# One-hots of four tokens in two VectorE operations, 64 expert tiles projected in the routing stage

## The chip, the core and the metric

The kernel runs on one core of one Trainium2 chip. A core has five engines with a queue each, and each works through its queue in order: TensorE (PE, with its weight loads shown apart as PEld), VectorE (DVE), ScalarE (ACT), GpSimd (POOL) and SyncE (SP), which here only issues transfers. The metric is the device time of one execution in microseconds.

## The reference

The program is two transformer blocks on 512 tokens of 1024 values. Only the last part of the second block, `peer`, is touched: each token picks, in each of 8 heads, 16 of 16384 experts by two lists of 128 sub-keys, and adds up what these experts give.

```
q = (xb @ w_query).reshape(TOKEN_BLOCK, P_HEADS, 2, P_HALF)
s = jnp.einsum('thpk,hpnk->thpn', q, sub_keys)
sv, si = lax.top_k(s, P_TOPK)
cand = sv[:, :, 0, :, None] + sv[:, :, 1, None, :]
cidx = si[:, :, 0, :, None] * N_KEYS + si[:, :, 1, None, :]
fv, fpos = lax.top_k(cand.reshape(...), P_TOPK)
eidx = jnp.take_along_axis(cidx.reshape(...), fpos, axis=-1)
g = jax.nn.softmax(fv, axis=-1)
act = jax.nn.gelu(jnp.einsum('td,thkd->thk', xb, u_tab[eidx]))
return jnp.einsum('thk,thkd->td', g * act, v_tab[eidx])
```

## The kernel before

Tokens stand in 4 tiles of 128. Tile 0 (NG = 1) is "gathered": for each of its 128 choices the rows of the tables `peer_u` and `peer_v` are fetched by an indirect DMA and used on VectorE (256 steps, `g_load` and `g_use`, lines 1607 to 1621). The other 3 tiles (ND = 3) are computed dense: for each of 128 tiles of 128 experts, all 384 tokens are projected (24 matmuls of 384 columns in three-term split precision, `mm3`, lines 196 to 198), put through gelu, weighted by a dense matrix of routing weights, and multiplied with the `peer_v` tile into PSUM (`acc`).

Three stages follow one another.

The **top-16 stage** ends with VectorE picking the 16 best sub-keys (lines 1536 to 1540).

The **routing stage** makes the weights, and beside it TensorE already projects NPRE of the 128 expert tiles. Its parts:
- `fill(n)` projects one expert tile ahead ("fill tile"): a load of `ur`, two casts `uh` on ScalarE (line 1720), two differences `ul` on GpSimd (line 1723), 24 matmuls, a gelu, and a write of the result `ga` to DRAM (`gad`, line 1745).
- `route(T)` finds the final 16 of each head for token tile T: a chain of about 80 VectorE instructions, with one exponential on ScalarE.
- `scatter(T)`, for the 3 dense tiles, turns the choices (row i, column j and weight of each) into dense weights. For each group of 4 tokens (32 groups a tile, 96 in all) it builds one-hot rows of i and j (`hots`, line 1898, two VectorE instructions), multiplies one of them with the weight in three bf16 parts (`part`, line 1904, on VectorE and GpSimd; `weigh`, line 1909, on ScalarE), forms the outer products (`outer`, line 1917, 12 matmuls of 128 x 128) and copies them to `stg` (`keep`, line 1924). After 16 groups `stg` is written to the DRAM tensor `gd_p` in four transfers (line 1944).

The **late stage** loops over the 128 expert tiles: it loads `vr` and the weights `gt` (line 1641, from `gd_p`), projects the tiles that are not done yet (`uh`, `ul` by lines 186 and 192), multiplies with `vr`, and spreads the 256 gather steps over the loop; a tile that is done ahead carries only GPRE = 0.36 of another's share of them.

The order in the routing stage is set by a planner, `Agenda`. Each piece of work is given an engine, a cost in us, the pieces that it needs and an aim (the time at which it should run). The planner plays this through and emits on each engine, whenever it is free, the ready piece with the earliest aim; buffers (`bufs`: two pairs `uh`/`ul`, three `ur`, OHB = 3 sets of one-hots, two `sc` banks) hold a piece back until an older user is through. What it emits is the order of each queue; on the chip the queues wait for one another by semaphores.

Of the kernel before, what the change touches and what calls it, by code (L numbers as in the profile page):

```python
# [1477 lines left out]
NPRE = 52  # L1478
LEAD, EACH, TOTAL = 36.0, 70.0, 275.0
# [11 lines left out]
def peer(kk, out):  # L1491
# [206 lines left out]
    quad = stp.tile([128, 128, 4], BF, name="quad")  # L1698
    nc.gpsimd.tensor_copy(quad, iota[:, :, None].to_broadcast([128, 128, 4]))
    ag = Agenda()  # L1700
    bufs = {"ur": 3, "u": 2, "mm": 3, "ga": 4, "sc": 2, "oh": OHB, "stg": 2}
    def fill(n):
        e, aim = pre[n], n * TOTAL / NPRE
        st = {}

        def load():
            st["raw"] = u_load(e)

        if n < len(early):
            st["raw"], ld = early[n], None  # L1710
        else:
            ld = ag.add("SP", 0, load, aim=aim - 12, nbytes=128 * D * 4, ring=[("ur", n)])
        los = []
        for q in range(2):
            sl = slice(q * 4, q * 4 + 4)

            def hi(sl=sl, q=q):
# [8 lines left out]
            t = ag.add("ACT", 0.52, hi, [ld], aim, ring=ring)
            if n % LOPOOL:
                los.append(ag.add("DVE", 0.62, lambda f=lo: f(nc.vector), [t], aim, ring=ring))
            else:
                los.append(ag.add("POOL", 1.25, lambda f=lo: f(nc.gpsimd), [t], aim, ring=ring))  # L1730
        for s_ in range(4):
            def mms(s_=s_):
                if s_ == 0:
# [5 lines left out]
            t = ag.add("PE", 0.96, mms, [los[s_ // 2]], aim + 3 + s_, ring=[("u", n), ("mm", n)])  # L1739
# [4 lines left out]
        t = ag.add("ACT", 0.38, act, [t], aim + 6, ring=[("mm", n), ("ga", n)])
        ag.add("SP", 0, lambda: nc.sync.dma_start(gad[:, e, :], st["ga"]), [t], aim + 6,
               nbytes=128 * ND * 128 * 4, ring=[("ga", n)])

    def route(T, aim, span, start):
# [26 lines left out]
        step("DVE", 1.2, begin)  # L1775
# [16 lines left out]
        for i in range(0, 8, 2):  # L1792
            step("DVE", 1.4, lambda i=i: best(i))
# [8 lines left out]
        step("DVE", 0.35, weights)  # L1802
# [46 lines left out]
        step("DVE", 2.7, column)  # L1849
        step("DVE", 1.15, lambda: pick(st["ge"], st["ge"], st["di"]))  # L1850
        step("DVE", 1.15, lambda: pick(st["tm"], st["tm"], st["s2"]))
        step("DVE", 1.4, lambda: tree(st["res"][:, 0, :], st["ge"]))
# [10 lines left out]
    def scatter(T, done, aim, span):  # L1863
# [9 lines left out]
        def turned():  # L1873

            v = st["ps"][:, :384].rearrange("p (a n) -> p a n", a=3)
            st["ij"] = tk.tile([128, 2, 128], BF, name="ij", tag="ij", bufs=1)
# [1 line left out]
            w = [tk.tile([128, 128], BF, name=f"w{c}", tag=f"w{c}", bufs=1) for c in range(3)]
            r = [tk.tile([128, 128], FT, name=f"wr{c}", tag=f"wr{c}", bufs=1) for c in range(2)]
            st["w"] = w + r[1:]  # L1880
            nc.scalar.copy(r[0], v[:, 2, :])
# [8 lines left out]
        ready = ag.add("DVE", 0.8, lambda: None, [ready], aim)  # L1890
        evs = []
        for g in range(32):
            t0 = aim + span * g / 32
# [36 lines left out]
            t = []  # L1930
            for c, lo, hi, eng in ((1, 0, WPOOL, "POOL"), (1, WPOOL, 4, "DVE"), (0, 0, 4, "DVE"), (2, WACT, 4, "DVE")):
                if lo < hi:
                    cost = 0.05 + 0.27 * (hi - lo) if eng == "POOL" else 0.07 + 0.07 * (hi - lo)
                    t.append(ag.add(eng, cost, lambda f=part, c=c, lo=lo, hi=hi, e=eng:
                                    f(nc.gpsimd if e == "POOL" else nc.vector, c, lo, hi), [u], t0, ring=[o1]))
            if WACT:
                t.append(ag.add("ACT", 0.3 * WACT, weigh, [u], t0, ring=[o1]))
# [220 lines left out]
```

## Time and profile before

| | us |
|---|---|
| median of 3 runs | 2541.49 (2539.76 to 2541.68) |
| the profiled execution | 2541.76 |
| its span in the trace | 2540.0 |
| routing stage, first fill matmul to first `acc` matmul | 1284.7 to 1691.5 |
| late stage, to the last gather steps | 1691.5 to 2490 |
| TensorE busy in the span | 2442.7 (96%) |
| VectorE busy in the span | 1910.8 (75%) |
| GpSimd busy in the span | 679.6 (27%) |

All times of the trace count from the start of the span. A matmul's duration in the trace contains its latency; consecutive ones overlap, so what it costs TensorE is the distance from its start to the next start. "Busy" is the share of time in which at least one instruction of the engine is under way. [...]

### The profile page before, as it was taken

What the parts mean: (1) busy time and instruction counts of PE and PEld (TensorE: products, weight loads), DVE (VectorE), ACT (ScalarE), POOL (GpSimd) and SP (SyncE); (2) the same over time, 40 slices, a digit from 0 to 9 for tenths busy, and PEclk for the clock granted to TensorE, in tenths of its full rate; (3) what the DMA queues carried; (4) which work ended last, traced back from release to release, by engine and by line L of the source; (5) the groups of instructions that cost most, each with busy time, mean ns of one, the idle gap of its engine ahead of it and who ended that gap; (6) DMA issues with size and microseconds to landing.
All of it is one profiled execution on the core that took longest, in us unless ns stands there. A gap on an engine that the chain in (4) does not pass through costs nothing.

```text
span 2540.0 us, 36035 instructions
## 1 busy us (share of the span) xinstructions
PE 2442.7 (96%) x12979; PEld 2121.0 (84%) x12979; DVE 1910.8 (75%) x3886; ACT 1079.0 (42%) x1887; POOL 679.6 (27%) x599
## 2 busy tenths in 40 slices
PE   5989999999999999999989999999999999999998
PEld 4778877887888887778888888988888888888887
DVE  7655655676665565576899998849889889999987
ACT  3444544442332365565236676832332223322333
POOL 3110010120000020004335565544333333433330
PEclk9999999999999999999999999999999999999999
DMA  7533243546554222224133454499999999999992
GB/s 251 150 123 108 84 150 112 175 142 207 179 185 137 76 74 76 67 68 156 61 95 100 174 185 158 150 346 361 336 347 333 331 346 337 341 334 335 348 351 95
DMA packets 295715, 506.84 MB, mean 200 GB/s; under 512 B 20871, under 2 KB 193521, under 8 KB 292209
## 3 DMA queue, kind: packets, MB, share of 16 engines
q1 hardware_dynamic: 257104, 367.96, 44.1%
q0 software_dynamic: 36864, 134.23, 14.1%
q8 instruction: 102, 1.67, 0.3%
q10 hardware_dynamic: 1568, 2.35, 0.3%
q14 instruction: 77, 0.62, 0.1%
HBM read 460.70 MB, written 43.78 MB: 199 GB/s over the span
## 4 chain that ended last, share of the span: by engine, by line
PE 80%; DVE 14%; DMA 2%; issue 2%; ACT 2%; POOL 0%; DVEq 0%; ACTq 0%; SPq 0%; POOLq 0%
PE mm L197 16%; PE mm L198 16%; PE mm L196 16%; PE acc L196 7%; PE acc L198 7%; PE acc L197 7%; PE sc L1917 3%; DVE oh L1904 2%; DVE oh L1898 2%; PE av L813 1%; PE sc L926 1%; PE av L940 1%; DMA adraw<-in_w_ada 1%; PE sc L794 1%; PE sc L1549 1%
## 5 line engine op out<-in xcount | busy, mean ns | idle before, releaser
L196 PE MATMUL mm<-hh,wh 128*128 128x512 f32 (+2 forms) x976 | 373.3, 384 | 5.0 <-ACT hh L519 3.4
L197 PE MATMUL mm<-hl,wh 128*128 128x512 f32 (+2 forms) x976 | 371.6, 381 | 2.4 <-DVE hl L331 2.4
L198 PE MATMUL mm<-hh,wl 128*128 128x512 f32 (+2 forms) x976 | 370.3, 380 | 1.4 <-DVE wl L192 1.4
L196 PE MATMUL mm<-hh,uh 128*128 128x384 f32 x1024 | 353.6, 345 | 4.5 <-ACT uh L186 4.5
L198 PE MATMUL mm<-hh,ul 128*128 128x384 f32 x1024 | 347.5, 339 | 0.2
L197 PE MATMUL mm<-hl,uh 128*128 128x384 f32 x1024 | 346.8, 339 | 0.0
L186 ACT CAST wh<-wraw 128x1024 fp32r<-128x1024 f32 (+1 forms) x170 | 173.6, 1026 | 364.0 <-PE mm L197 331.8
L196 PE MATMUL acc<-vh,wgh 128*128 128x512 f32 x768 | 301.1, 392 | 0.0
L198 PE MATMUL acc<-vh,wgl 128*128 128x512 f32 x768 | 300.1, 391 | 0.0
L197 PE MATMUL acc<-vl,wgh 128*128 128x512 f32 x768 | 298.6, 389 | 0.0
L186 ACT CAST vh<-vr 128x1024 fp32r<-128x1024 f32 x128 | 135.2, 1056 | 235.6 <-PE acc L198 230.0
L192 DVE TENSOR_TENSOR wl<-wraw,wh 128x1024 fp32r<-128x1024 f32 x135 | 171.6, 1272 | 78.5 <-ACT wh L186 71.8
L1607 POOL DMA_INDIRECT gr<-in_peer_v,widx x128 | 159.0, 1242 | 252.3 <-DVE gacc L1621 214.6
L1592 ACT ACTIVATE ga<-mm 128x384 f32<-128x384 f32 x128 | 64.8, 506 | 370.4 <-PE mm L198 357.2
L1607 POOL DMA_INDIRECT gr<-in_peer_u,widx x128 | 152.1, 1188 | 242.4 <-DVE gacc L1613 221.0
L196 PEld LDWEIGHTS mm<-hh,wh 128*128 128x128 f32 (+1 forms) x976 | 183.2, 188 | 39.2 <-ACT hh L519 3.9
L197 PEld LDWEIGHTS mm<-hl,wh 128*128 128x128 f32 (+1 forms) x976 | 183.6, 188 | 36.2 <-DVE hl L331 3.4
L198 PEld LDWEIGHTS mm<-hh,wl 128*128 128x128 f32 (+1 forms) x976 | 183.7, 188 | 35.1 <-DVE wl L192 1.8
L196 PEld LDWEIGHTS mm<-hh,uh 128*128 128x128 f32 x1024 | 196.2, 192 | 8.2 <-ACT uh L186 5.2
L197 PEld LDWEIGHTS mm<-hl,uh 128*128 128x128 f32 x1024 | 195.3, 191 | 3.4
L198 PEld LDWEIGHTS mm<-hh,ul 128*128 128x128 f32 x1024 | 194.5, 190 | 0.9 <-DVE ul L192 0.9
L1723 POOL TENSOR_TENSOR ul<-ur,uh 128x512 fp32r<-128x512 f32 x104 | 146.2, 1418 | 130.5 <-ACT uh L1720 124.2
(500 smaller groups left out, 5094.8 us busy)
## 6 DMA issues: line engine op xcount, KB each, us to landing
ur<-in_peer_u_t SPq DMA_DIRECT2D x128, 512.0 KB, 6.0
vr<-in_peer_v SPq DMA_DIRECT2D x128, 512.0 KB, 5.3
wraw<-in_w_fc SPq DMA_DIRECT2D x32, 1024.0 KB, 5.6
adraw<-in_ada_w SPq DMA_DIRECT2D x96, 256.0 KB, 3.0
gd_p<-stg SPq DMA_DIRECT2D x24, 1024.0 KB, 7.0
gt<-gd_p SPq DMA_DIRECT2D x64, 384.0 KB, 7.0
wraw<-in_w_in SPq DMA_DIRECT2D x33, 512.0 KB, 3.8
adraw<-in_w_ada SPq DMA_DIRECT2D x64, 256.0 KB, 2.8
```

The source lines that it names most:

```text
L186: nc.scalar.copy(hi, view)
L192: eng.tensor_tensor(lo, view, hi, OP.subtract)
L196: nc.tensor.matmul(out, a[0], b[0], start=first, stop=False)
L197: nc.tensor.matmul(out, a[0], b[1], start=False, stop=False)
L198: nc.tensor.matmul(out, a[1], b[0], start=False, stop=last)
L794: nc.tensor.matmul(sc[:, i * n:(i + 1) * n], qp[g, hh][:, q0:q0 + 128], k_[:, :n], start=a == 0, stop=a == 1)
L1592: nc.scalar.activation(ga, ps, AF.Gelu)
L1607: nc.gpsimd.indirect_dma_start(out=r, out_offset=None, in_=A[tab], in_offset=bass.IndirectOffsetOnAxis(ap=widx[t][:, k:k + 1], axis=0))
L1723: eng.tensor_tensor(st["u"][1][:, sl, :], st["raw"][:, sl, :], st["u"][0][:, sl, :], OP.subtract)
L1898: nc.vector.tensor_tensor(o[i], quad, st["ij"][:, i, None, g * 4:g * 4 + 4].to_broadcast([128, 128, 4]), OP.is_equal)
L1904: eng.tensor_tensor(o[2 + c][:, :, lo:hi], o[0][:, :, lo:hi], w, OP.mult)
L1917: nc.tensor.matmul(ps[:, q * 128:(q + 1) * 128], o[2 + c][:, :, q], o[1][:, :, q], start=c == 0, stop=c == 2)
```

## The change

The one-hots of a group of 4 tokens are held as two pairs of tokens, with the two tokens of a pair innermost, for i and j together. One VectorE instruction of 1024 elements per partition compares them (`hots`), a second of 1536 elements multiplies all three weight parts (`parts`); `part` and `weigh`, and with them GpSimd's and ScalarE's share, are gone. In `outer` the unweighted one-hot of i is now the stationary operand and the weighted one of j streams; the step between its columns is 4 bytes where it was 8. The differences `ul` of the fill tiles move from GpSimd to VectorE. 64 tiles instead of 52 are projected in the routing stage; the first 16 have aims 4.2 us apart. Token tile 0 is routed last instead of second. Most costs that the planner is given are new numbers too.

```diff
@@
-NPRE = 52
-LEAD, EACH, TOTAL = 36.0, 70.0, 275.0
+NPRE = 64
+LEAD, EACH, TOTAL = 36.0, 100, 310
+NLEAD, PACE = 16, 4.2
...
-OHB, WACT, WPOOL = 3, 2, 2
-GPOS = 1
+OHB = 3
+GPOS = 3
...
-    quad = stp.tile([128, 128, 4], BF, name="quad")
-    nc.gpsimd.tensor_copy(quad, iota[:, :, None].to_broadcast([128, 128, 4]))
+    twice = stp.tile([128, 128, 2], BF, name="twice")
+    nc.gpsimd.tensor_copy(twice, iota[:, :, None].to_broadcast([128, 128, 2]))
...
+    def fill_aim(n):
+
+        return n * PACE if n < NLEAD else NLEAD * PACE + (n - NLEAD) * (TOTAL - NLEAD * PACE) / (NPRE - NLEAD)
+
     def fill(n):
-        e, aim = pre[n], n * TOTAL / NPRE
+        e, aim = pre[n], fill_aim(n)
...
-            t = ag.add("ACT", 0.52, hi, [ld], aim, ring=ring)
-            if n % LOPOOL:
-                los.append(ag.add("DVE", 0.62, lambda f=lo: f(nc.vector), [t], aim, ring=ring))
-            else:
-                los.append(ag.add("POOL", 1.25, lambda f=lo: f(nc.gpsimd), [t], aim, ring=ring))
+            t = ag.add("ACT", 0.62, hi, [ld], aim, ring=ring)
+            los.append(ag.add("DVE", 0.7, lo, [t], aim, ring=ring))
...
-            st["ij"] = tk.tile([128, 2, 128], BF, name="ij", tag="ij", bufs=1)
-            nc.scalar.copy(st["ij"], v[:, 0:2, :])
...
+            ij = st["ij"] = tk.tile([128, 64, 2, 2], BF, name="ij", tag="ij", bufs=1)
+            w3 = st["w3"] = tk.tile([128, 64, 3, 2], BF, name="w3", tag="w3", bufs=1)
...
+            def of(v, g):
+                return v[:, 2 * g:2 * g + 2, :, None, :].to_broadcast([128, 2, v.shape[2], 128, 2])
+
             def hots(g=g):
...
-                for i in range(2):
-                    nc.vector.tensor_tensor(o[i], quad, st["ij"][:, i, None, g * 4:g * 4 + 4].to_broadcast([128, 128, 4]),
-                                            OP.is_equal)
...
-            def part(eng, c, lo, hi, g=g):
...
-                eng.tensor_tensor(o[2 + c][:, :, lo:hi], o[0][:, :, lo:hi], w, OP.mult)
-
-            def weigh(g=g):
...
-                for q in range(WACT):
-                    nc.scalar.activation(o[4][:, :, q], o[0][:, :, q], AF.Copy,
-                                         scale=st["w"][3][:, g * 4 + q:g * 4 + q + 1])
+                o = st["oh", g] = stp.tile([128, 2, 2, 128, 2], BF, name="oh", tag="oh", bufs=OHB)
+                nc.vector.tensor_tensor(o, twice[:, None, None, :, :].to_broadcast([128, 2, 2, 128, 2]), of(st["ij"], g),
+                                        OP.is_equal)
+
+            def parts(g=g):
+                o = st["ow", g] = stp.tile([128, 2, 3, 128, 2], BF, name="ow", tag="ow", bufs=OHB)
+                nc.vector.tensor_tensor(o, st["oh", g][:, :, 1, None, :, :].to_broadcast([128, 2, 3, 128, 2]),
+                                        of(st["w3"], g), OP.mult)
...
-                        nc.tensor.matmul(ps[:, q * 128:(q + 1) * 128], o[2 + c][:, :, q], o[1][:, :, q],
+                        nc.tensor.matmul(ps[:, q * 128:(q + 1) * 128], o[:, q // 2, 0, :, q % 2], w[:, q // 2, c, :, q % 2],
                                          start=c == 0, stop=c == 2)
...
-            u = ag.add("DVE", 0.74, hots, [ready], t0, ring=[o1])
...
-            t = ag.add("PE", 0.68, outer, t, t0, ring=[o1, o2])
+            u = ag.add("DVE", 0.7, hots, [ready], t0, ring=[o1])
+            t = ag.add("DVE", 0.97, parts, [u], t0, ring=[o1])
+            t = ag.add("PE", 0.72, outer, [t], t0, ring=[o1, o2])
```

The places where the queues differ most follow, as the instructions stand on each engine.

VectorE at the start of the routing stage, before: `sv` and `si` are the top-16 work, `h2r` an unrelated sum, `cand` the first piece of `route`.

```order
L1681 TENSOR_TENSOR h2r_10156<-h2r_10156,sc 128x512
L1539 MAX sv_10173<-s_11137 128x8
L1761 CAST si_10175<-si_10175 128x256
L1540 MAX_INDEX si_10177<-sv_10173,s_11137 128x8
L1768 TENSOR_TENSOR cand<-sv_10171 128x8x16
```

The same place now:

```order
L1681 TENSOR_TENSOR h2r_10156<-h2r_10156,sc 128x512
L1539 MAX sv_10170<-s_11137 128x8
L1727 TENSOR_TENSOR ul<-ur,uh 128x512
L1540 MAX_INDEX si_10174<-sv_10170,s_11137 128x8
L1727 TENSOR_TENSOR ul<-ur,uh 128x512
L1681 TENSOR_TENSOR h2r_10156<-h2r_10156,sc 128x512
L1762 CAST si_10175<-si_10175 128x256
L1769 TENSOR_TENSOR cand<-sv_10171 128x8x16
```

The first `ul` of the first fill tile stands behind all but one of the top-16 instructions; before, it was GpSimd's, which had nothing else to do.

VectorE on one group of 4 tokens late in the stage, before: `oh_15799` and `oh_15800` are the one-hots of i and j, the next three the weighted parts.

```order
L1898 TENSOR_TENSOR oh_15799<-quad_11149,ij_14702 128x512
L1898 TENSOR_TENSOR oh_15800<-quad_11149,ij_14702 128x512
L1904 TENSOR_TENSOR oh_15802<-oh_15799,w1_14705 128x128x2
L1904 TENSOR_TENSOR oh_15801<-oh_15799,w0_14704 128x512
L1904 TENSOR_TENSOR oh_15803<-oh_15799,w2_14706 128x128x2
```

The same place now, with the two `ul` of a fill tile between the groups:

```order
L1727 TENSOR_TENSOR ul_15456<-ur_15292,uh_15455 128x512
L1906 TENSOR_TENSOR ow_15476<-oh_15465,w3_14463 128x1536
L1727 TENSOR_TENSOR ul_15456<-ur_15292,uh_15455 128x512
L1901 TENSOR_TENSOR oh_15508<-twice_11149,ij_14462 128x1024
L1906 TENSOR_TENSOR ow_15510<-oh_15508,w3_14463 128x1536
```

Five VectorE instructions a group became two larger ones, and the fill tiles' `ul` joined the queue.

SyncE at the end of the routing stage, before: `gd_p<-stg` writes the dense weights, `gt<-gd_p` is the first read of them, `gad<-ga` and `ur` belong to fill tiles.

```order
L1944 DMA gd_p<-stg 128x2048
L1745 DMA gad<-ga 128x384
L1509 DMA ur<-in_peer_u_t 128x1024
L1944 DMA gd_p<-stg 128x2048
L1745 DMA gad<-ga 128x384
L1509 DMA ur<-in_peer_u_t 128x1024
L1745 DMA gad<-ga 128x384 x3
L1509 DMA ur<-in_peer_u_t 128x1024 x2
L1638 DMA vr<-in_peer_v 128x1024
L1641 DMA gt<-gd_p 128x6x128
```

The same place now:

```order
L1934 DMA gd_p<-stg 128x2048
L1509 DMA ur<-in_peer_u_t 128x1024 x2
L1746 DMA gad<-ga 128x384
L1509 DMA ur<-in_peer_u_t 128x1024
L1746 DMA gad<-ga 128x384 x2
L1934 DMA gd_p<-stg 128x2048 x4
L1638 DMA vr<-in_peer_v 128x1024
L1641 DMA gt<-gd_p 128x6x128
```

The last four writes of the weights stood among fill tiles; now they stand together, directly ahead of the first read. TensorE's queue has the matching move: behind the last outer product stood seven whole fill tiles (168 matmuls) and the late stage's first two projections (48 matmuls); now all 64 fill tiles stand ahead of the last seven groups (84 matmuls), and only the 48 matmuls follow before the first `acc`.

## Rows read from the trace of the kernel before

**Rows 1.** Stretches: us; busy us and instructions by engine, PEclk, DMA share, GB/s

```profile
1285.00:1645.00 360.00, 334.38 (x2232) 316.95 (x2232) 335.76 (x942) 245.87 (x440) 203.54 (x187) 0.98 0.44 149
1645.00:1690.00 45.00, 40.26 (x223) 38.79 (x222) 4.28 (x6) 16.41 (x31) 21.12 (x18) 0.96 0.88 317
1690.00:2490.00 800.00, 800.00 (x3942) 711.66 (x3941) 722.14 (x1019) 242.13 (x348) 305.25 (x250) 1.00 0.97 341
```

**Rows 2.** Timeline of TensorE, fill matmuls: start us, us, engine, line, operation

```profile
1284.73 0.42 PE L196 MATMUL mm<-hh,uh 128*128 128x384 f32 x1
...
1673.68 0.34 PE L196 MATMUL mm<-hh,uh 128*128 128x384 f32 x1
...
1675.59 0.34 PE L198 MATMUL mm<-hh,ul 128*128 128x384 f32 x1
```

**Rows 3.** Timeline of TensorE: outer products with six fill matmuls between

```profile
1626.53 1.58 PE L1917 MATMUL sc<-oh 128*128 128x128 bf16 x12
...
1628.99 1.58 PE L1917 MATMUL sc<-oh 128*128 128x128 bf16 x12
```

**Rows 4.** Instructions of the tile `acc`: ns min/median/max, first to last start us

```profile
L196 PE MATMUL acc<-vh,wgh x768: 387/389/478, 1691.5 to 2530.3; 128*128 128x512 f32 x192
```

**Rows 5.** Timeline of TensorE, three pauses: [idle before, who ended it]

```profile
1319.43 0.47 PE L1871 MATMUL sc<-ident,res 128*128 128x128 f32 x1 [4.87 <-DVE res L1841]
...
1322.08 0.52 PE L197 MATMUL mm<-hl,uh 128*128 128x384 f32 x1
...
1685.27 0.44 PE L196 MATMUL mm<-hh,uh 128*128 128x384 f32 x1 [3.44 <-ACT uh L186]
```

**Rows 6.** Groups of VectorE, 1285 to 1645 us: count | busy us, mean ns

```profile
L1898 DVE TENSOR_TENSOR oh<-quad,ij 128x512 bf16<-128x512 bf16 x192 | 101.3, 576 | 8.8 <-PE sc L1917 8.1 <-POOL oh L1904 0.5
L1904 DVE TENSOR_TENSOR oh<-oh,w 128x256 bf16<-128x256 bf16 x192 | 83.1, 448 | 0.0
L1904 DVE TENSOR_TENSOR oh<-oh,w 128x512 bf16<-128x512 bf16 x96 | 55.9, 582 | 0.0
```

**Rows 7.** Timeline, VectorE alone, then beside GpSimd

```profile
1327.55 0.74 DVE L1898 TENSOR_TENSOR oh<-quad,ij 128x512 bf16<-128x512 bf16 x2
...
1397.12 2.76 POOL L1723 TENSOR_TENSOR ul<-ur,uh 128x512 fp32r<-128x512 f32 x2 [0.90 <-ACT uh L1720]
1397.23 2.93 DVE L1898 TENSOR_TENSOR oh<-quad,ij 128x512 bf16<-128x512 bf16 x2
```

**Rows 8.** Chain of waits: a 2048-element bf16 operation of VectorE: start us, us

```profile
1339.93 1.14 DVE tm L1812
```

**Rows 9.** Groups of VectorE, 1690 to 2490 us: two float32 differences

```profile
L192 DVE TENSOR_TENSOR vl<-vr,vh 128x1024 fp32r<-128x1024 f32 x122 | 148.8, 1220 | 11.7 <-ACT vh L186 11.0 <-DMA vr<-in_peer_v 0.7
L192 DVE TENSOR_TENSOR ul<-ur,uh 128x512 fp32r<-128x512 f32 x143 | 98.3, 687 | 44.1 <-ACT uh L186 43.6 <-DMA vr<-in_peer_v 0.5
```

**Rows 10.** Timeline at the stage's start: GpSimd's first `ul`, VectorE's last top-16 instruction

```profile
1284.86 2.54 POOL L1723 TENSOR_TENSOR ul<-ur,uh 128x512 fp32r<-128x512 f32 x2 [25.59 <-ACT uh L1720]
...
1293.49 0.28 DVE L1540 FIND_INDEX8 si<-sv,s 128x8 uint32<-128x128 f32 x1
```

**Rows 11.** ScalarE's copy of the outer products, 1285 to 1676 us

```profile
L1924 ACT COPY stg<-sc 128x512 f32<-128x512 f32 x96 | 106.0, 1111 | 47.8 <-PE sc L1917 47.2
```

**Rows 12.** Transfers of the tile `gd_p`, writes and reads: issue to landing, us

```profile
DMA to landing us min/median/max: 3.9/7.0/15.0
```

**Rows 13.** Timeline: the first read of `gd_p`, and VectorE's first use of it

```profile
1678.41 0.61 SPq L1641 DMA_DIRECT2D gt<-gd_p  x1
...
1690.05 0.55 DVE L1989 TENSOR_TENSOR gt<-gt,ga 128x384 f32<-128x384 f32 x1
```

**Rows 14.** Weight loads of the outer products (line 1917): ns min/median/max

```profile
L1917 PEld LDWEIGHTS <-oh x1152: 112/117/138, 1333.6 to 1646.4; 128*128 128x128 bf16 x192
```

**Rows 15.** Stretches of the late stage with the most bytes; columns as in rows 1

```profile
1690.00:1730.00 40.00, 40.00 (x207) 36.75 (x206) 39.28 (x65) 13.54 (x21) 17.53 (x14) 1.00 1.02 375
...
2410.00:2450.00 40.00, 40.00 (x202) 35.74 (x201) 37.29 (x46) 10.84 (x16) 17.58 (x14) 1.00 1.06 375
```

More of the change, by code (lines that the diff above doesn't have):

```diff
@@ L1738, in mms @@
                            k == 0, k == KD - 1)
[L1739 removed]
+            t = ag.add("PE", 1.05, mms, [los[s_ // 2]], aim + 3 + s_, ring=[("u", n), ("mm", n)])
         def act():
             st["ga"] = u_gelu(st["ps"])
[L1744 removed]
+        t = ag.add("ACT", 0.5, act, [t], aim + 6, ring=[("mm", n), ("ga", n)])
         ag.add("SP", 0, lambda: nc.sync.dma_start(gad[:, e, :], st["ga"]), [t], aim + 6,
@@ L1773, in begin @@
             st["fp"] = tk.tile([128, 8, 16], U32, name="fp", tag="fp", bufs=1)
-        step("DVE", 1.2, begin)
+        step("DVE", 1.3, begin)
         def best(i0):
@@ L1792, in route @@
         for i in range(0, 8, 2):
-            step("DVE", 1.4, lambda i=i: best(i))
+            step("DVE", 2.3, lambda i=i: best(i))
         def weights():
@@ L1800, in weights @@
             nc.vector.tensor_copy(st["pb"].rearrange("p (k h) -> p h k", h=8), st["fp"])
-        step("DVE", 0.35, weights)
+        step("DVE", 0.75, weights)
         step("ACT", 1.5, lambda: nc.scalar.activation(st["g"], st["g"], AF.Exp))
@@ L1807, in rows @@
             nc.vector.tensor_tensor(st["ge"], st["pb"][:, None, :].to_broadcast([128, 16, 128]), wide[0], OP.is_ge)
-        step("DVE", 1.15, rows)
+        step("DVE", 1.22, rows)
         def pick(out, t, v):
@@ L1817, in offset @@
             pick(st["tm"], st["ge"], dst)
-        step("DVE", 1.15, offset)
+        step("DVE", 1.22, offset)
         def norm():
@@ L1832, in norm @@
             nc.vector.tensor_copy(st["s2"], st["si2"][:, 1].rearrange("p h r -> p r h"))
-        step("DVE", 1.0, norm)
+        step("DVE", 1.7, norm)
         def tree(out, src):
@@ L1847, in column @@
             nc.vector.tensor_tensor(st["tm"], st["pb"][:, None, :].to_broadcast([128, 16, 128]), wide[1], OP.is_equal)
[L1849 to L1852, printed above, removed]
+        step("DVE", 3.1, column)
+        step("DVE", 1.22, lambda: pick(st["ge"], st["ge"], st["di"]))
+        step("DVE", 1.22, lambda: pick(st["tm"], st["tm"], st["s2"]))
+        step("DVE", 1.6, lambda: tree(st["res"][:, 0, :], st["ge"]))
         def end():
@@ L1856, in end @@
             routed[T] = st["res"]
-        step("DVE", 1.4, end)
+        step("DVE", 1.6, end)
         for i, (eng_, cost, fn) in enumerate(steps):
@@ L1875, in turned @@
             v = st["ps"][:, :384].rearrange("p (a n) -> p a n", a=3)
-            st["ij"] = tk.tile([128, 2, 128], BF, name="ij", tag="ij", bufs=1)
-            nc.scalar.copy(st["ij"], v[:, 0:2, :])
[L1878 to L1881, printed above, removed]
-            for c in range(2):
-                nc.vector.tensor_copy(w[c], r[c and 1])
-                nc.vector.tensor_tensor(r[1], r[c and 1], w[c], OP.subtract)
-            nc.vector.tensor_copy(w[2], r[1])
+            ij = st["ij"] = tk.tile([128, 64, 2, 2], BF, name="ij", tag="ij", bufs=1)
+            w3 = st["w3"] = tk.tile([128, 64, 3, 2], BF, name="w3", tag="w3", bufs=1)
+            r = [tk.tile([128, 64, 2], FT, name=f"wr{c}", tag=f"wr{c}", bufs=1) for c in range(2)]
+            for c in range(2):
+                nc.scalar.copy(ij[:, :, c, :], v[:, c, :].rearrange("p (n t) -> p n t", t=2))
+            nc.scalar.copy(r[0], v[:, 2, :].rearrange("p (n t) -> p n t", t=2))
+            for c in range(2):
+                nc.vector.tensor_copy(w3[:, :, c, :], r[c and 1])
+                nc.vector.tensor_tensor(r[1], r[c and 1], w3[:, :, c, :], OP.subtract)
+            nc.vector.tensor_copy(w3[:, :, 2, :], r[1])
         s0 = sc0 + a * 33
@@ L1889, in scatter @@
         ready = ag.add("ACT", 0.7, turned, [first], aim, ring=[("sc", s0)])
-        ready = ag.add("DVE", 0.8, lambda: None, [ready], aim)
+        ready = ag.add("DVE", 1.3, lambda: None, [ready], aim)
         evs = []
@@ L1928, in scatter @@
             o1, o2 = ("oh", n), ("sc", s0 + 1 + g)
-            u = ag.add("DVE", 0.74, hots, [ready], t0, ring=[o1])
[L1930 to L1937, printed above, removed]
-            t = ag.add("PE", 0.68, outer, t, t0, ring=[o1, o2])
+            u = ag.add("DVE", 0.7, hots, [ready], t0, ring=[o1])
+            t = ag.add("DVE", 0.97, parts, [u], t0, ring=[o1])
+            t = ag.add("PE", 0.72, outer, [t], t0, ring=[o1, o2])
             r = ("stg", 2 * a + g // 16)
-            evs.append(ag.add("ACT", 0.48, keep, [t], t0, ring=[o2, r]))
+            evs.append(ag.add("ACT", 1.1, keep, [t], t0, ring=[o2, r]))
             if g % 16 == 15:
```

11 lines of the change are left out of this document (3 added, 8 removed).

## The prediction

> **What bounds the kernel now.** I read the table of stretches first. In the late stage TensorE is busy 800 of 800 us: there only fewer matmuls help. In the routing stage TensorE has 334 of 360 us, VectorE 336 and GpSimd 204, so neither of the two main queues is full, and each waits for the other at times [rows 1]. Next come the distances on TensorE's timeline. Eleven consecutive fill matmuls start 1675.59 - 1673.68 = 1.91 us apart, 0.1736 us each [rows 2], so a fill tile of 24 costs 4.17 us. From one group's outer products to the next, with six fill matmuls between, it is 2.46 us [rows 3]; less 6 x 0.1736 that leaves 1.42 us for a group, 0.118 a matmul.
>
> The routing stage runs from the first fill matmul, 1284.73 [rows 2], to the first `acc` at 1691.5 [rows 4]: 406.8 us. TensorE's work in it is 52 x 24 + 48 = 1296 fill matmuls, 225.0 us, and 96 x 1.42 = 136.3 us of outer products: 361.3. The remaining 45.5 us are some 3 us of transposes and, for the rest, waiting: for `route`, which also leaves TensorE at half clock for a while (0.52 us a fill matmul for 0.34), for one-hots, and at the end for `uh` [rows 5].
>
> **The frame of the sum.** Twelve more tiles bring 288 x 0.1736 = 50.0 us of matmuls into the routing stage and take the same out of the late stage. On a busy TensorE that cancels. So time after = 2541.76 + (X - 45.5) + Y, with X the new remainder of the routing stage and Y new waiting of TensorE in the late stage. The profiled execution is 0.27 us above the median, and I take that off at the end.
>
> **VectorE's work.** The one-hots go: 101.3 + 83.1 + 55.9 = 240.3 us [rows 6]. Two operations of 512 took 0.74 us with GpSimd idle and 2.93 us beside GpSimd's `ul` [rows 7], so part of those 240 us was mutual hindrance, which ends, as no GpSimd tensor operation is left in the stage. For the new ones: 0.37 us per 512 elements [rows 7] and 1.14 us for 2048 bf16 elements [rows 8] give a slope of 0.26 per 512. That makes `hots` (1024) about 0.63 and `parts` (1536) 0.88: 1.51 us a group, 145 us for 96. The upper bound is float32 at about one element a cycle: 1220 ns for 1024, 687 for 512 [rows 9], so 1220 + 1753 = 2.97 us a group, 285 us. I take 1.51, since the nearest rows are bf16 with the same kind of broadcast operand. The fill tiles' `ul` cost 128 x 0.687 = 88 us more. VectorE: 336 - 240 + 145 + 88 = 329 us against 361.3 + 50.0 = 411 us of TensorE. TensorE is now the slower queue by far, so most waits for one-hots inside the stage should go. ScalarE loses `weigh` and keeps the copy of 1.11 us a group [rows 11], under the 1.42.
>
> What speaks against the price is the innermost run of two. [...]
>
> **Outer products.** Their step between columns falls from 8 to 4 bytes. The weight loads take 117 ns each [rows 14], which is the pace of 118: these seem to bound the group, not the 128 streamed columns. I keep 1.42 us. The other end is the pace of fill matmuls scaled to 128 columns, 0.1736 / 3 = 0.058: 1152 x (0.118 - 0.058) = 69 us less. Upwards I see no reason, as the load has the same 128 columns and a smaller step.
> [...]
>
> **X, term by term.**
> - Transposes: 3 us.
> - Start. GpSimd did the first `ul` at 1284.86, at once; VectorE's last top-16 instruction runs until 1293.8 [rows 10]. The first `ul` now stands behind that work, and each third matmul needs it, so TensorE stops after the first ones: about 1285.2 to 1293.2, 8 us. It has idled that long, so some fill matmuls follow at half clock: 8 x 0.18 = 1.5 us. Bounds 0 (VectorE reaches its `ul` early) and 10.
> - First scatter: 2 us, as `route` still takes longer than the fill tiles allotted to it last (4.87 us of waiting before [rows 5]). Later pauses: 5 us, between 0 (TensorE always behind its plan) and 20 (half of what it was).
> - End. All fill tiles now stand ahead of the last seven groups, and 48 matmuls, 8.3 us, are all that is left behind the last outer product. Then come: copy 1.1 [rows 11], issue 0.6 [rows 13], four transfers of 1.05 MB that wait for that copy, 4.2 MB / 341 GB/s [rows 1] = 12.3 us, reading `gt` 7.0 (the median landing [rows 12]), two VectorE steps of 0.55 [rows 13]. That is 22.1 us, 13.8 of them uncovered, plus 1.5 at half clock. Before, seven fill tiles stood there and covered it. Bounds: the least landing, 3.9 [rows 12], for writing and for reading leaves about 2 us; 15.0 for writing and 11.6 for reading (1678.41 to 1690.05 [rows 13]) leave 21.
>
> X = 3 + 8 + 1.5 + 2 + 5 + 13.8 + 1.5 = 34.8, so 10.7 us less than 45.5. By the bounds, X is 3 + 0 + 0 + 0 + 2 = 5 to 3 + 11.5 + 2 + 20 + 22.5 = 59.
>
> **Y.** The late stage moved 341 GB/s x 800 us = 273 MB [rows 1]. Twelve tiles done ahead load `ga` (0.197 MB) in place of `ur` (0.524): 3.9 MB less. 269 MB in 750 us are 359 GB/s. Two stretches of 40 us ran at 375 with TensorE never waiting [rows 15], so it can be met; VectorE has 722 - 12 x 2 x 0.687 = 706 of 750 us, 94%. I take Y = 2 us, with 0 and 29 as bounds (the third rival).
> Sum: 2541.76 - 10.7 + 2 = 2533.1; less the 0.27 us that the profiled execution stands above the median, 2532.8, about 2533.
>
> **Rivals.**
> 1. The outer products get faster with the smaller step. For it: nothing in the rows says why a load of 128 bf16 columns takes 117 ns, and the fill matmuls show that 128 columns stream in 58. Against: the load [rows 14] is the same in length. With a half to all of 69 us gone from TensorE, VectorE's 329 us are still below the stage, but waits come back: some 40 us less, 2493.
> 2. The one-hots run at an element a cycle. Then VectorE has 336 - 240 + 285 + 88 = 469 us against 411, and the stage is VectorE's: 469 + 8 + 13.8 + about 5 of `route`'s latency = about 496, less 406.8 + 50.0: 39 us more, and 2 of Y: 2582. Against it stand rows 7 and 8.
> 3. On the slower side: the late stage becomes bound by transfers. They need 359 GB/s for 750 us, and the rows show 375 only for 40 us at a time and 341 on average, at a DMA share of 0.97 [rows 1, 15]. At 345 GB/s the 269 MB take 779 us: Y = 29, and 2533 + 27 = 2560. It decides against the change from 269 / (750 + 11) = 353 GB/s down. For it: each tile done ahead is 4.17 us of `acc` matmuls, and with its loads and its 0.36 share it asks for more bytes per us than a full tile. Against it: the gather steps ran to 2490 with no pause of TensorE at all, so nothing shows that the average was a limit.
> That the change doesn't do what it says can only be in part: GpSimd's operations are gone from the code; if they weren't what held VectorE up, that is rival 2.
>
> **Chances.** A measurement here tells about 0.2%, 5 us, from no change. The forecast has 0.57; its own range is 2514 to 2549 (X of 16 to 51). Of that, 0.41 are below 2536, 0.13 within 5 us of 2541.5, and 0.03 above. Rival 1 has 0.14, all faster. Rival 2 has 0.09, all slower. Rival 3 has 0.20: 0.18 slower, 0.02 same. Together: faster 0.55, same 0.15, slower 0.30. The range of 8 in 10 runs from 2490, with most of rival 1 in, to 2561, with most of rival 3 in and rival 2 left out.
>
> **What the next profile would show.** Right: a gap of some 8 us on TensorE from 1285, ended by VectorE's `ul`; `hots` near 0.65 and `parts` near 0.9 us; weight loads still at 117 ns; few pauses for one-hots; a gap behind the last outer product of 10 to 15 us, ended by `gt`; TensorE without idle time in the late stage, at about 359 GB/s. Wrong: `hots` at 1.2 us (rival 2), weight loads near 60 to 80 ns (rival 1), idle time of TensorE behind `vr`, `ur` or `weights` in the late stage (rival 3).

## The result and the profile after

| | before | after |
|---|---|---|
| median, us | 2541.37 (4 runs) | 2474.08 (2471.45 to 2478.51, 4 runs) |
| span of the profiled execution, us | 2540.0 | 2470.6 |
| routing stage, us | 406.8 | 387.0 |
| first to last `acc` start of line 196, us | 838.8 | 790.5 |

The ratio is 0.9736 (95% interval 0.9724 to 0.9748): 67 us faster, where 9 were forecast; the time lies outside the range of 2490 to 2561.

The stretches of the kernel after, with the columns of [rows 1] (PEclk is the granted TensorE clock as a share of its full speed):

```profile
1283.00:1645.00 362.00, 345.95 (x2700) 332.07 (x2698) 314.52 (x774) 205.85 (x308) 2.07 (x2) 0.98 0.57 188
1645.00:1670.00 25.00, 10.44 (x48) 9.80 (x48) 5.29 (x9) 5.69 (x11) 3.77 (x4) 0.74 0.98 379
1670.00:2420.00 750.00, 749.97 (x3643) 661.25 (x3644) 701.42 (x986) 222.74 (x310) 305.19 (x250) 1.00 0.99 356
```

The late stage is as full as before (TensorE busy 749.97 of 750 us), and transfers run at 356 GB/s there. The routing stage holds 12 more tiles and is yet 20 us shorter. Its TensorE timeline shows why; eighteen fill matmuls stand between the two rows, and [rows 3] answer to them:

```profile
1625.22 0.86 PE L1914 MATMUL sc<-ow,oh 128*128 128x128 bf16 x12
...
1629.12 0.86 PE L1914 MATMUL sc<-ow,oh 128*128 128x128 bf16 x12
```

3.90 us less 18 x 0.1736 leaves 0.775 us for a group where it was 1.42: over 96 groups 62 us. The twelve matmuls take 0.86 us from the first start to the last end, 1.58 before. The instructions of line 1914 and of the tile `acc` (ns min/median/max, first to last start us; [rows 14] and [rows 4] answer):

```profile
L1914 PEld LDWEIGHTS <-oh x1152: 96/97/145, 1334.0 to 1643.5; 128*128 128x128 bf16 x192
L1914 PE MATMUL sc<-ow,oh x1152: 217/218/308, 1334.0 to 1643.5; 128*128 128x128 bf16 x192
...
L196 PE MATMUL acc<-vh,wgh x768: 389/389/767, 1670.0 to 2460.5; 128*128 128x512 f32 x192
```

Consecutive outer products now start 57 ns apart in the median of the 1152, for 118 before, though a recorded weight load still lasts 97. VectorE's groups, 1283 to 1645 us (count | busy us, mean ns | idle before; [rows 6]):

```profile
L1906 DVE TENSOR_TENSOR ow<-oh,w 128x1536 bf16<-128x1536 bf16 x96 | 89.7, 955 | 0.2
L1727 DVE TENSOR_TENSOR ul<-ur,uh 128x512 fp32r<-128x512 f32 x128 | 85.6, 688 | 30.3 <-ACT uh L1724 30.3
L1901 DVE TENSOR_TENSOR oh<-twice,ij 128x1024 bf16<-128x1024 bf16 x96 | 64.1, 685 | 10.2 <-PE sc L1914 10.1
```

And what TensorE waited for in the stage, from 1283 to 1671 us (us in total, times, longest):

```profile
PE acc L196 <- ACT ga L1592: 14.2, 1, 14.2
PE sc L1914 <- DVE ow L1906: 8.0, 4, 3.8
PE mm L198 <- DVE ul L1727: 6.4, 1, 6.4
PE mm L196 <- ACT uh L186: 1.6, 1, 1.6
```

### The profile page after: what moved, and what is told of

Its sections match the earlier page's. It is cut to its first block, busy times and chain, and to the rows that moved or that the text cites. A ratio compares the mean times of both kernels' runs of the same rounds, so it can differ in the third digit from the quotient of the medians.

```text
span 2470.6 us, 35338 instructions
## 1 busy us (share of the span) xinstructions
PE 2374.7 (96%) x12979; PEld 2056.2 (83%) x12979; DVE 1876.5 (76%) x3702; ACT 1010.4 (41%) x1698; POOL 458.8 (19%) x399
## 4 chain that ended last, share of the span: by engine, by line
PE 88%; DVE 6%; DMA 2%; ACT 2%; issue 1%; POOL 0%; DVEq 0%; ACTq 0%; SPq 0%; POOLq 0%
PE mm L196 18%; PE mm L197 18%; PE mm L198 18%; PE acc L196 7%; PE acc L198 7%; PE acc L197 7%; PE sc L1914 3%; PE av L813 1%; PE sc L926 1%; PE av L940 1%; DMA adraw<-in_w_ada 1%; DMA gt<-gd_p 1%; PE sc L1549 1%; PE sc L794 1%; PE sc L394 1%
## 5 line engine op out<-in xcount | busy, mean ns | idle before, releaser
L196 PE MATMUL acc<-vh,wgh 128*128 128x512 f32 x768 | 301.5, 393 | 14.2 <-ACT ga L1592 14.2
L196 PEld LDWEIGHTS acc<-vh,wgh 128*128 128x128 f32 x768 | 144.5, 188 | 41.8 <-ACT ga L1592 14.4
```

What stands on the lines that cost most here:

```text
L196: nc.tensor.matmul(out, a[0], b[0], start=first, stop=False)
```

## The experiments

One theory stood at the start, with two rivals. Step: the outer products sped up because the columns of an operand are nearer (8 to 4 bytes). Reuse: the stationary operand is now the same for three matmuls running. GpSimd: it no longer works beside TensorE. Each ratio below is to the kernel before on the same chip; e2, e3, e9, e10 and e11 are single executions.

**The old layout in the new kernel (e1).** One tile of four tokens innermost in place of the two pairs, for both operands, `twice` and the index tiles likewise:

```diff
-                o = st["oh", g] = stp.tile([128, 2, 2, 128, 2], BF, name="oh", tag="oh", bufs=OHB)
+                o = st["oh", g] = stp.tile([128, 2, 128, 4], BF, name="oh", tag="oh", bufs=OHB)
...
-                o = st["ow", g] = stp.tile([128, 2, 3, 128, 2], BF, name="ow", tag="ow", bufs=OHB)
+                o = st["ow", g] = stp.tile([128, 3, 128, 4], BF, name="ow", tag="ow", bufs=OHB)
```

> The changed kernel with the one-hots laid out four tokens innermost again (columns of an operand 8 bytes apart, as before the change); still two VectorE operations a group, the same order of operands, the same plan. Theory step: the pace of the outer products is set by the step between an operand's columns. Then 12 of them take 1.34 us again instead of 0.67, 96 x 0.67 = 64 us come back on a TensorE that is the full queue, and the time is about 2474 + 62 = 2536 (2525 to 2541). Rival reuse: the pace fell because the stationary operand now stays the same over three matmuls. Then 0.67 us and 2474 remain. Rival GpSimd: it fell because GpSimd no longer works beside TensorE. Then also 0.67 us and 2474.

Measured: 2538.53 us, ratio 0.9984 (0.9974 to 0.9994). A group on TensorE's timeline:

```profile
1500.72 1.58 PE L1913 MATMUL sc<-ow,oh 128*128 128x128 bf16 x12
```

The pace is 118 ns again, with hardly any GpSimd work beside the groups (busy 0.0 of the 360 us from 1285 to 1645) and the stationary operand the same for three matmuls: both rivals fall. `hots` and `parts` keep 685 and 954 ns, so this is the change less the step alone, and it is worth 4 us.

**Which operand (e2, e3).** Only the layout of one of the two tiles goes back to four innermost. e2:

```diff
-                o = st["ow", g] = stp.tile([128, 2, 3, 128, 2], BF, name="ow", tag="ow", bufs=OHB)
+                ow = stp.tile([128, 3, 128, 4], BF, name="ow", tag="ow", bufs=OHB)
+                o = st["ow", g] = ow.rearrange("p c n (u t) -> p u c n t", t=2)
```

> As the changed kernel, but only the streamed operand (the weighted one-hots) has its columns 8 bytes apart; the stationary one keeps 4. Theory step of the streamed operand: 118 ns a matmul, as before the change. Rival step of the stationary operand: 57 ns, as in the changed kernel. The write of the one-hots may be slower in this layout (VectorE over 0.95 us), so the pace of consecutive matmuls decides, not the time.

e3, with the one-hots of i and j in a tile of four and the weighted ones in pairs:

```diff
-                o = st["oh", g] = stp.tile([128, 2, 2, 128, 2], BF, name="oh", tag="oh", bufs=OHB)
+                o = st["oh", g] = stp.tile([128, 2, 128, 4], BF, name="oh", tag="oh", bufs=OHB)
...
+                w = st["ow", g] = stp.tile([128, 2, 3, 128, 2], BF, name="ow", tag="ow", bufs=OHB)
+                o = w.rearrange("p u c n t -> p c n u t")
```

> As the changed kernel, but only the stationary operand (the unweighted one-hots) has its columns 8 bytes apart; the streamed one keeps 4. Theory step of the streamed operand: 57 ns a matmul. Rival step of the stationary operand: 118 ns, and weight loads of 117 ns instead of 97. If both count: between, in this run and in the one with the streamed operand.

Measured: 117 ns with the streamed operand at 8 bytes (e2, 2536.85 us), 60 ns with the stationary one (e3, 2496.59 us). Timeline of TensorE, a group of 12 in e2, then in e3:

```profile
1405.80 1.56 PE L1915 MATMUL sc<-ow,oh 128*128 128x128 bf16 x12
```

```profile
1407.91 0.90 PE L1916 MATMUL sc<-ow,oh 128*128 128x128 bf16 x12 [0.20 <-DVE ow L1907]
```

The weight loads in e2, where the pace is 117 ns, and in e3, where it is 60:

```profile
L1915 PEld LDWEIGHTS <-oh x1152: 96/117/134, 1340.3 to 1708.5; 128*128 128x128 bf16 x192
```

```profile
L1916 PEld LDWEIGHTS <-oh x1152: 110/113/149, 1335.8 to 1667.1; 128*128 128x128 bf16 x192
```

So the step of the streamed operand it is. In e3 a recorded load of 113 ns does not keep the pace from being 60: the loads overlap there, and the length of a record is not the cost. In e2 the stationary tile is that of the change, where a load lasted 97 ns; only the streamed operand differs, and the loads' records are 117 ns again. There the record follows the pace and does not set it. e3's time is not that of the step: with its order of elements `parts` took 1573 ns for 955, and TensorE waited 15.3 us for it from 1283 to 1694 us, for 8.0 in the change.

**How the pace goes with the step (e9, e10, e11).** e9 and e10 pad each pair of the streamed operand (e10 with 8 for 3, and OHB = 2):

```diff
-                o = st["ow", g] = stp.tile([128, 2, 3, 128, 2], BF, name="ow", tag="ow", bufs=OHB)
+                o = st["ow", g] = stp.tile([128, 2, 3, 128, 3], BF, name="ow", tag="ow", bufs=OHB)[:, :, :, :, 0:2]
```

> As the changed kernel, with one unused bf16 value between the pairs of the streamed operand, so that its columns stand 6 bytes apart (VectorE writes with that step too). Theory in proportion to the step: 57 ns a matmul at 4 bytes, 118 at 8, so about 88 here. Rival threshold: 57 or 118, nothing between.

> As the changed kernel, with six unused values behind each pair of the streamed operand, so that its columns stand 16 bytes apart, and two sets of one-hots instead of three for space. Theory in proportion to the step: 118 ns at 8 bytes, so about 236 here. Rival: a column costs one access or two, whatever the distance; then 118 as at 8 bytes.

e11 keeps each token's one-hots apart (tiles of 4 x 2 x 128 and 4 x 3 x 128, a plain row of indices in place of `twice`):

```diff
-                nc.vector.tensor_tensor(o, twice[:, None, None, :, :].to_broadcast([128, 2, 2, 128, 2]), of(st["ij"], g),
+                nc.vector.tensor_tensor(o, once[:, None, None, :].to_broadcast([128, 4, 2, 128]), of(st["ij"], g),
```

> As the changed kernel, with each token's one-hots apart: columns of both operands 2 bytes apart, but the innermost run of the compared and of the weight operand is one value read again and again. [...] VectorE, by the one-element bound of the prediction: hots 1.22 and parts 1.75 us instead of 0.68 and 0.95, 128 us more on VectorE in the stage, which then is the bound: about 2474 + 90 to 120. Rival: VectorE keeps 0.68 and 0.95 (a value read again is no hindrance) and the time stays 2474.

| step of the streamed columns, bytes | 2 (e11) | 4 (after) | 6 (e9) | 8 (e1) | 16 (e10) |
|---|---|---|---|---|---|
| median ns from one matmul to the next | 56 | 57 | 88 | 118 | 230 |

A group of 12 on TensorE's timeline in e11, e9 and e10:

```profile
1501.66 0.84 PE L1914 MATMUL sc<-ow,oh 128*128 128x128 bf16 x12 [0.93 <-DVE ow L1906]
```

```profile
1505.94 1.21 PE L1914 MATMUL sc<-ow,oh 128*128 128x128 bf16 x12
```

```profile
1512.20 2.90 PE L1914 MATMUL sc<-ow,oh 128*128 128x128 bf16 x12
```

In these runs it is 14.3 to 14.8 ns a byte of step from 4 bytes to 16, in proportion; 2 bytes gain nothing more (56 ns for 57). Both forecasts of the proportion held. The times are mixed with other costs: 2506.84 (e9), 2698.77 (e10), 2570.65 (e11), as VectorE's writes with these steps slowed too (`parts` 1474 ns in e9 and 1540 in e10, for 951 in the change). In e11 VectorE is the bound, groups from 1283 to 1800 us:

```profile
L1906 DVE TENSOR_TENSOR ow<-oh,w 128x1536 bf16<-128x1536 bf16 x96 | 166.6, 1757 | 0.2
L1901 DVE TENSOR_TENSOR oh<-once,ij 128x1024 bf16<-128x1024 bf16 x96 | 115.0, 1220 | 0.0
```

These are the 1.75 and 1.22 us that the prediction set as the upper bound, and rival 2's world: of the layouts run here, the pair of tokens innermost is the one that has VectorE fast (955 and 685 ns) and TensorE's columns near (57 ns) at once.

**The step alone in the kernel before (e4, e5).** The five old tiles hold pairs. In e4 the instructions go through the elements in the old order, in e5 in the order of memory. The line of e5 (e4 adds a view of the same tile in the old order):

```diff
-                o = st["ab", g] = [stp.tile([128, 128, 4], BF, name="oh", tag=f"oh{i}", bufs=OHB) for i in range(5)]
+                o = st["ab", g] = [stp.tile([128, 2, 128, 2], BF, name="oh", tag=f"oh{i}", bufs=OHB) for i in range(5)]
```

> The kernel before with one thing changed: its five one-hot tiles hold two pairs of tokens, two tokens innermost, so that columns of either operand are 4 bytes apart; the same nine one-hot instructions on the same engines, same order of operands, same plan, 52 tiles ahead. Theory step: 57 ns a matmul instead of 118, 96 x 0.67 = 64 us less on TensorE; but VectorE with 336 of 360 us becomes the bound, so only some 15 to 25 us are gained: 2516 to 2526. Rivals reuse and GpSimd: 118 ns and 2541 (or later, where the one-hot instructions get slower with a run of two).

> The kernel before with one thing changed, this time without a slower order of the elements on VectorE: its five one-hot tiles hold two pairs of tokens with two tokens innermost, and each instruction goes through its tile in the order in which it lies in memory. Same instructions, engines, operands and plan, 52 tiles ahead. Theory step plus VectorE: 57 ns a matmul instead of 118, 64 us less work on TensorE, but VectorE (336 of 360 us in the stage before) then is the bound and TensorE waits for one-hots, so 2516 to 2541. Rival (the step alone is the change's whole gain): about 2541 - 64 = 2477.

e4: 2561.42 us, ratio 1.0073 (1.0055 to 1.0091), 0.7% slower: matmuls at 58 ns, but `hots` at 725 ns for 576 in [rows 6], so its expectation missed. e5: 2536.45 us, 0.9973 (0.9964 to 0.9983), as forecast. TensorE has some 64 us less work (a group of 12 takes 0.86 us, as in the change) and hardly anything is gained; its waits for one-hots in the kernel before, then in e5, 1283 to 1700 us:

```profile
PE sc L1917 <- DVE oh L1904: 15.0, 18, 2.1
...
PE sc L1917 <- POOL oh L1904: 2.7, 1, 2.7
```

```profile
PE sc L1921 <- DVE oh L1908: 41.6, 34, 2.8
PE sc L1921 <- POOL oh L1908: 16.0, 5, 4.3
```

These waits are 40 us longer, and the granted clock from 1285 to 1640 us is 0.94 on average for 0.98 before. The step alone is worth 6 us (e5), the rest alone 4 us (e1), the two together 67.

**Twelve tiles less (e6) and `ul` back on GpSimd (e7).**

```diff
-NPRE = 64
+NPRE = 52
```

> The changed kernel with 52 tiles projected ahead instead of 64 (aims spread over the same time). Theory cancel: 12 tiles cost TensorE 50 us in either stage; TensorE stays the full queue in both, the time stays within 4 us of 2474. Rival VectorE: with outer products of 0.67 us the routing stage has TensorE work of 225 + 67 = 292 us, less than VectorE's 314 - 17 = 297 and its waits, so without the 12 tiles TensorE idles for one-hots: 2484 to 2505.

```diff
-                nc.vector.tensor_tensor(st["u"][1][:, sl, :], st["raw"][:, sl, :], st["u"][0][:, sl, :], OP.subtract)
+                nc.gpsimd.tensor_tensor(st["u"][1][:, sl, :], st["raw"][:, sl, :], st["u"][0][:, sl, :], OP.subtract)
...
-            los.append(ag.add("DVE", 0.7, lo, [t], aim, ring=ring))
+            los.append(ag.add("POOL", 1.25, lo, [t], aim, ring=ring))
```

> The changed kernel with the fill tiles' differences on GpSimd again (planned at 1.25 us each); the rest as changed. Theory hindrance: VectorE loses 88 us of its own, but its one-hots stretch beside GpSimd (0.37 us per 512 elements alone, 1.46 beside it), hots to over 1 us and parts to over 1.4 us on average, so that VectorE gains little; the gap of 6.4 us at the start of the stage goes. Time 2465 to 2485. Rival no hindrance: hots stays at 0.68 and parts at 0.95, VectorE is relieved by 88 us, waits for one-hots (8 us) and the gap at the start (8 us) go: about 2458.

e6: 2488.66 us, ratio 0.9787 (0.9771 to 0.9804), 0.0051 above the change's 0.9736, some 13 us. The cancelling that the prediction counted on fails, and the time lies where rival VectorE had it. The stage takes 1287.4 to 1635.6, 348 us: 39 less, not 50. TensorE's waits in it:

```profile
PE acc L196 <- ACT ga L1592: 16.2, 1, 16.2
PE sc L1914 <- DVE ow L1906: 9.3, 6, 3.1
PE mm L198 <- DVE ul L1727: 8.9, 5, 6.4
PE sc L1914 <- ACT stg L1921: 3.7, 4, 1.6
```

Of the 9 us that they are longer than in the change, 3.8 are put down to VectorE, 3.2 to ScalarE's copy and 2.0 to the end of the stage; it is not shown that VectorE alone holds TensorE up.

e7: 2494.02 us, 0.9811 (0.9795 to 0.9827), 19 us worse than the change and worse than its own forecast. VectorE's groups in e7:

```profile
L1906 DVE TENSOR_TENSOR ow<-oh,w 128x1536 bf16<-128x1536 bf16 x96 | 121.3, 1280 | 1.0
L1901 DVE TENSOR_TENSOR oh<-twice,ij 128x1024 bf16<-128x1024 bf16 x96 | 91.6, 970 | 18.3 <-PE sc L1914 18.2
```

The 86 us of `ul` gone from VectorE came back as 59 us of stretched one-hots (1280 for 955, 970 for 685), and TensorE waited 19.8 us for them, in 17 waits, for 8.0 in the change.

**Both ends mended (e8).** The first two fill tiles' `ul` on GpSimd, the last six fill tiles aimed behind the last group, the first `vr` and `gt` issued as soon as the queue has the writes:

```diff
+        if n >= NPRE - NEND:
+            return 340.0 + 4.2 * (n - NPRE + NEND)
...
-            def lo(sl=sl):
-                nc.vector.tensor_tensor(st["u"][1][:, sl, :], st["raw"][:, sl, :], st["u"][0][:, sl, :], OP.subtract)
+            def lo(sl=sl, eng=nc.gpsimd if n < 2 else nc.vector):
+                eng.tensor_tensor(st["u"][1][:, sl, :], st["raw"][:, sl, :], st["u"][0][:, sl, :], OP.subtract)
...
-            los.append(ag.add("DVE", 0.7, lo, [t], aim, ring=ring))
+            los.append(ag.add(*(("POOL", 1.25) if n < 2 else ("DVE", 0.7)), lo, [t], aim, ring=ring))
...
-            ag.add("SP", 0, lambda it=it: load_v(it), end, aim + 50 + it, nbytes=128 * D * 4, ring=ring)
+            ag.add("SP", 0, lambda it=it: load_v(it), (), aim + VAIM + it, nbytes=128 * D * 4, ring=ring, after=end)
```

> The changed kernel with its two ends mended: the first two fill tiles' differences on GpSimd, the last 6 fill tiles planned behind the last group, and the first reads for the late stage issued ahead of their writes. Theory ends: the gap of 6.4 us at the start with 1.5 us at half clock goes, and the 14.2 us and 4 us at half clock behind the last outer product are covered by 120 more fill matmuls (20.9 us): 2474 - 8 - 15 = 2451 (2446 to 2460). Rival VectorE: the stage's length is set by VectorE's one-hots, so fill tiles moved behind them leave TensorE idle earlier: the gaps move, and 2465 to 2475 is left.

Measured: 2455.52 us, ratio 0.9660 (0.9644 to 0.9676), 19 us below the change and the fastest here. TensorE's waits, 1283 to 2450 us:

```profile
PE sc L1917 <- DVE ow L1909: 6.9, 3, 3.8
PE mm L196 <- ACT uh L1727: 3.5, 1, 3.5
PE mm L198 <- DVE ul L1730: 1.6, 4, 0.5
```

The waits of 14.2 and 6.4 us are gone. What each of the three edits gave was not tried apart.

**80 tiles ahead (e12)**, in e8's kernel, aims stretched (EACH 120, TOTAL 372, the last six at 400):

> The kernel with mended ends, with 80 tiles ahead instead of 64 (aims stretched alike). Theory cancel: 16 tiles move 66.7 us of TensorE from the late stage to the routing stage; the time stays within 5 us of 2455. Rival late stage: with 683 us left for some 264 MB (386 GB/s, where 356 was the mean seen) and VectorE needing 701 - 16 x 1.37 = 679 of 683 us, TensorE begins to wait there: at 356 GB/s 741 us, 2455 + 58 = 2513; by VectorE alone 2460 to 2480.

Measured: 2466.18 us, ratio 0.9699 (0.9683 to 0.9715), 10 us more than e8. From the first to the last `acc` of line 196 e12 takes 735.7 us, e8 788.6: 52.9 less, where 66.7 us of matmuls are gone, so the late stage lost 14 us. Its stretch, with the columns of [rows 1]:

```profile
1740.00:2420.00 680.00, 677.39 (x3191) 575.24 (x3190) 656.71 (x925) 193.91 (x254) 304.30 (x242) 1.00 1.02 374
```

VectorE is busy 97% there and transfers run at 374 GB/s; e8 had 93% and 348 GB/s in this stretch. The time falls where the expectation had VectorE (2460 to 2480); the price by transfers, 2513, assumed 356 GB/s, which was exceeded. The trace says which of the two decides. TensorE's short pauses stand almost all ahead of the first matmuls of a tile; here, in the timeline, it starts 0.50 us after the matmul before, for 0.23 elsewhere:

```profile
2096.37 0.40 DVE L188 CAST wgh<-gt 128x384 fp32r<-128x384 f32 x1
...
2096.42 0.39 PE L198 MATMUL acc<-vh,wgl 128*128 128x512 f32 x1
...
2096.92 0.47 PE L196 MATMUL acc<-vh,wgh 128*128 128x512 f32 x1
```

It waits for `wgh`, which VectorE has only just made (2096.37 + 0.40 = 2096.77). VectorE's own waits from 1740 to 2420 us (those above 0.15 us) are two:

```profile
DVE vl L192 <- ACT vh L186: 2.2, 1, 2.2
DVE wg L1620 <- ACT gact L1619: 0.4, 1, 0.4
```

VectorE waits 2.6 us in 680, so it is VectorE's own work that holds TensorE up in this stretch, not the transfers.

## Why the prediction was wrong

**The outer products (the step that failed).** The prediction kept 1.42 us a group because "the weight loads take 117 ns each, which is the pace of 118: these seem to bound the group". They don't: e3 ran at 60 ns with loads of 113. Two equal numbers were read as cause. A row of the kernel before would have warned, the weight loads of the fill matmuls:

```profile
L196 PEld LDWEIGHTS mm<-hh,uh x1024: 186/188/332, 1284.7 to 2518.0; 128*128 128x128 f32 x171
```

188 ns recorded, at a pace of 174 [rows 2]: there, too, the record is longer than the pace, so these loads overlap and the record is not the cost. What was left unlooked at was the other operand. 128 columns of the fill's streamed operand go by in 58 ns (174 / 3) at 4 bytes a column; the outer product's stood 8 bytes apart and took twice that. The term was 96 x 1.42; it measures 96 x 0.775, 62 us less. That is near the lower end that the text had named (69 us), and it is the world of rival 1, which had 0.14. Its price was cut to 40 us for waits on VectorE, so its 2493 is 19 us too high; nearly all of the 62 us was kept, as in the change VectorE has 320 us of work to 349 of TensorE.

**The rest of the sum.** With the old pace put back, e1 measures 2538.5 us for the forecast of 2533. By terms, in the change:

| term | forecast | measured |
|---|---|---|
| X, stage less 275.0 us of fill matmuls less outer products (74.4) | 34.8 | 387.0 - 349.4 = 37.6 |
| wait for the first `ul` | 8 | 6.4 |
| waits for one-hots (forecast: later pauses and first scatter) | 5 + 2 | 8.0 |
| end, uncovered | 13.8 | 14.2 |
| Y, late stage | 2 | 790.5 - (838.8 - 50.0) = 1.7 |
| `hots`, `parts`, ns | 630, 880 | 685, 955 |
| VectorE in the stage | 329 | 319.8 |

VectorE's total is near by luck: the one-hots took 154 us for 145, the rest of its work beside `ul` 80 for 96. The end of the stage is near by luck too: the sum is right and its parts are not. The chain of waits of the kernel after, start us, us:

```profile
1642.93 1.92 ACT stg L1921 x2
...
1644.86 7.49 DMA gd_p<-stg
...
1652.41 13.80 DMA gt<-gd_p
...
1667.07 0.48 ACT ga L1592
...
1670.03 0.77 PE acc L196
```

The read waits for one of the four writes only, 7.5 us, not for all (12.3), and then takes 13.8 itself, not 7.0. From 1652.4 to 1666.2 us, the time of this read, transfers ran at 409 GB/s with a DMA share of 1.03, for 313 and 0.88 in the 7.5 us before: other writes of `gd_p` (the last landed 17.1 us after its issue) and gathered rows (13.4 us in the median) were under way beside it. That these made it slower is an estimate from this. The name in the list of waits (`ga`) is the last link of this chain, not the cause.

The start shows the clock as foreseen: after the gap fill matmuls take 0.52 us until 1294.96, and the granted clock from 1290 to 1295 us is 0.50 (in the kernel before, behind the pause of 4.87 us [rows 5], it is 0.50 from 1322 to 1324). The sixteen matmuls from 1290.00 take 5.18 us for 2.78 at the usual pace: 2.4 us lost, where 1.5 were forecast.

```profile
1283.27 0.34 PE L197 MATMUL mm<-hl,uh 128*128 128x384 f32 x1
1290.00 0.69 PE L198 MATMUL mm<-hh,ul 128*128 128x384 f32 x1 [6.38 <-DVE ul L1727]
1290.48 0.52 PE L196 MATMUL mm<-hh,uh 128*128 128x384 f32 x1
...
1294.96 0.38 PE L198 MATMUL mm<-hh,ul 128*128 128x384 f32 x1
1295.18 0.34 PE L196 MATMUL mm<-hh,uh 128*128 128x384 f32 x1
```

The late stage's 1.7 us are the clock, too, and not the waiting that Y stood for: after the pause of 14.2 us the granted clock is 0.50 from 1670 to 1673 us, and the first nine matmuls lose 1.8 us (3.66 for 1.88 at the usual pace). e8, without the pause, has 788.6 us from the first to the last `acc`, where 838.8 - 50.0 is 788.8.

**"Twelve tiles cancel."** True only while TensorE is full in both stages. With outer products at 0.775 us and 52 tiles, TensorE has 225.0 + 74.4 = 299 us of work to 306 of VectorE (1285 to 1636 us), and e6 is 13 us slower than the change: part of the tiles' work fills idle time.

That token tile 0 is routed last was not tried apart.

**Rival 2** gave the one-hots the pace of the float32 differences of [rows 9], 1220 ns for 1024 values. "An element a cycle" is the author's name for it; no trace shows VectorE's clock. The rival is refuted by `hots` at 685 ns for 1024 with two values innermost, and e11 shows it to be right for the layout of one token: 1220 with one value read again. **Rival 3** did not come: 356 GB/s with no wait of TensorE, and at 374 in e12 the loss was VectorE's. (Its 4.17 us of `acc` matmuls for a tile is the figure of a fill tile; the 18 `acc` matmuls start 0.227 us apart, 4.1 us. Nothing rests on it.)

**The gain, then:** TensorE's 62 us come from the step. They can be had only since VectorE was relieved (two operations of 685 and 955 ns a group, GpSimd busy 2 of 362 us): with neither that nor the 12 tiles 6 us are left (e5), with `ul` back on GpSimd 48 of the 67 (e7). The 12 tiles give TensorE work to do meanwhile; without them alone 54 are left (e6).

## What to carry to other kernels

Here the streamed operand set the matmul's pace (57 ns at a step of 4 bytes, 118 at 8, with weight loads recorded at 97 and 117): look at the step between the streamed columns before blaming the weight load, and test a pace against a second pair of load and matmul on the same page. Where two engines are both nearly full, price an edit in pairs: here the one half was worth 6 us, the other 4, both 67. A wait that a change creates at a stage's ends can be covered by leaving independent work for it (19 us in e8, with the other two edits there).

## What the runs showed of the hardware

- 128 streamed bf16 columns of the outer products cost 56 ns at a step of 2 bytes (e11) and 57 at 4 (after), then in proportion to the step: 88 at 6 (e9), 118 at 8 (e1), 230 at 16 (e10). A step of 8 bytes of the stationary operand cost almost nothing (60 ns in e3).
- VectorE's bf16 operation that writes 1536 values in runs of two took, in the median, 951 ns with the steps of 4 bytes of the change and 952 with 8 (e2), but 1474 with 6 (e9) and 1540 with 16 (e10), and 1573 in e3's order. Why was not pursued.
- VectorE beside GpSimd: its bf16 operations took 955 and 685 ns with GpSimd busy 2 of 362 us (the change), 1280 and 970 with GpSimd busy 201 of 357 (e7).
- In the changed kernel's pause transfers ran at 379 GB/s over 25 us and TensorE's granted clock was 0.74 on average there. After the pause of 14.2 us it was 0.50 from 1670 to 1673 us; after that of 6.4 us, from 1290 to 1295.
